# A decoder step's gate/up projection as seven block products instead of eight, and the down projection as a stage of its own

## The chip, the core and the metric

The program runs on one core of a Trainium2 chip. A core has TensorE (matrix products, PE in the profile), VectorE (DVE), ScalarE (ACT) and GpSimd (POOL), which work beside each other on a memory of 128 partitions (SBUF), with eight banks of PSUM for TensorE's sums; SyncE (SP) issues DMAs here, as does ScalarE. The metric is the device time of one launch in microseconds; less is better. Three runs of the kernel before took 3131.83, 3137.9 and 3143.32 us, median 3137.9.

## The reference

One layer of a decoder for a prompt of 2048 tokens and for 8 x 4 decoded tokens, in float32: an input projection, three branches of windowed attention, a state-space mixer, an output projection, a gated feed-forward part, and norms. What matters here:

```python
h = x + mixed @ w_out
gu = rmsnorm(h, norm_ffn) @ w_gate_up            # [tokens, 1024] @ [1024, 2 * 2816]
y = h + (silu(gu[:, :2816]) * gu[:, 2816:]) @ w_down
y = rmsnorm(y, norm_final)
```

## The kernel before

The prompt goes through in two halves of 1024 tokens, each as two quarters of 512. `half_step` (from L1131) runs the mixers and the output projection of the first quarter (its rows go to hD in DRAM), then of the second, and then the feed-forward part for both. The 32 decoded tokens go with the second half.

TensorE computes in a shortened form of float32, so each operand is split into a high and a low part, and each product is three matmuls (`mm3`, L102 to L109): high x high, high x low, low x high. A strip of weights of 128 columns is split where it arrives (`wunit`, L82 to L97: the high part on ScalarE, the low one on VectorE), and so are the inputs: `norm_T` (L125) normalizes 128 rows, transposes them on TensorE (L141) and splits them (L143, L144) into the tiles xa, for the first quarter, and xb.

The feed-forward loop (from L1312) runs over 22 groups f of 128 of the 2816 columns. For each group, the gate strip and then the up strip are multiplied with all blocks of tokens, 8 x 3 matmuls a block: in the first half two blocks of 512, in the second two of 272 (512 prompt tokens and the decoded ones) and one of 512. ScalarE takes the gate's silu (L1325), VectorE multiplies by the up sums (L1348), and the product is split (L1349, L1350). `down` (L1283 to L1301) then multiplies it with 128 rows of w_down and adds the sums to the eight accumulator rows acc (L1299): for each f in the first half, for two at a time in the second. TensorE thus changes between gate/up and down all through the stage. The decoded tokens' mixers are cut into some 60 steps (`sample_steps`), and `beside` puts up to three of them beside each f of the first half. Copies of cache rows from DRAM to DRAM are issued one per f. The next quarter's input is made ahead of the last `down` of the first half, and the last `down` carries the final norm (`finals`).

The order on an engine follows from a scheduler that takes the instructions by their place in the program and by when their inputs are ready; PSUM banks are asked for by name ("mm", "s", "o", "t").

Of the kernel before, what the change touches and what calls it, by code (L numbers as in the profile page):

```python
# [33 lines left out]
def hybrid_step(ctx: ExitStack, tc: tile.TileContext, x_prompt, x_sample, cache_kv_d1, cache_kv_d4,  # L34
# [33 lines left out]
    qD = dram.tile([NS, 768], F, name="qD")  # L68

# [12 lines left out]
    def wunit(src, a, pool=None, more=None):  # L82
        """[128, a, 1024//a] of a weight, as an exact sum of two fp32r parts; more: the parts of further columns"""
# [5 lines left out]
        hi, lo = [pool.tile([128, 1072 if pool is wsp else 1024], R, name=s)[:, :w].rearrange("p (a c) -> p a c", a=a)  # L89
                  for s in ("hi", "lo")]  # L90
# [11 lines left out]
    def mm3(ps, pairs):  # L102
        """sum over the pairs ((sh, sl), (mh, ml)) of s.T @ m"""
# [77 lines left out]
    def sample_state(sp):  # L181
        """constants and intermediates of the decoded tokens"""
# [50 lines left out]
    def x_stage(qi, xnp, es, nb=2):  # L233
        """-> the tiles of a quarter's input, and what makes the i-th of its rows' tiles"""
# [48 lines left out]
    def mixers(qi, xh, xl, mix, rssd, cvp):  # L283
# [15 lines left out]
        def g1(hi, lo, raw, M=128):  # L299
            """the strip's columns of the projection, by blocks of tokens: (psum, first, number)"""  # L300
# [6 lines left out]
        # weights, in the order they are used; each is asked for ahead of its use  # L307
# [25 lines left out]
        # ---- attention  # L333
# [4 lines left out]
        def softmax(mask, nk, hd_of, stt):  # L338
            """rows of scores -> unnormalized weights, negated maxima and sums in stt"""
# [63 lines left out]
        def kout(src_of, dst):  # L403
            """128 columns of a branch's two key strips as rows of the output"""
# [57 lines left out]
            # values, tokens on partitions  # L462
# [24 lines left out]
            # units  # L487
# [46 lines left out]
            # rows of the output  # L534
# [21 lines left out]
        # ---- state-space part  # L556
# [128 lines left out]
        # ---- gate of the state-space part, and its norm  # L685
# [445 lines left out]
    def half_step(half, X, right):  # L1131
# [51 lines left out]
        if not smp:  # L1183
            junk = g2.tile([128, D], F, name="j3")
# [313 lines left out]
```

## Time and profile before

| | |
|---|---|
| median of three runs | 3137.9 us |
| span of the profiled execution | 3141.2 us |
| TensorE busy | 3083.8 us (98%) |
| VectorE, ScalarE, GpSimd busy | 1649.3, 1075.0, 74.9 us |
| feed-forward, first half (775 to 1608) | 833.0 us |
| feed-forward, second half (2361 to 3134) | 773.0 us |
| mean DMA rate | 104 GB/s |

Instructions on TensorE are pipelined: the length shown for one is more than the distance to the next start, and the distance is what it costs. The profiled execution's own time is its span of 3141.2 us, 3.3 us above the median of the runs. The mean granted clock of TensorE is 0.986 of full speed.

### The profile page before, as it was taken

What the parts mean: (1) busy time and instruction counts of PE and PEld (TensorE: products, weight loads), DVE (VectorE), ACT (ScalarE), POOL (GpSimd) and SP (SyncE); (2) the same over time, 40 slices, a digit from 0 to 9 for tenths busy, and PEclk for the clock granted to TensorE, in tenths of its full rate; (3) what the DMA queues carried; (4) which work ended last, traced back from release to release, by engine and by line L of the source; (5) the groups of instructions that cost most, each with busy time, mean ns of one, the idle gap of its engine ahead of it and who ended that gap; (6) DMA issues with size and microseconds to landing.
All of it is one profiled execution on the core that took longest, in us unless ns stands there. A gap on an engine that the chain in (4) does not pass through costs nothing.

```text
span 3141.2 us, 44468 instructions
## 1 busy us (share of the span) xinstructions
PE 3083.8 (98%) x18203; PEld 2538.0 (81%) x18203; DVE 1649.3 (53%) x3186; ACT 1075.0 (34%) x2139; POOL 74.9 (2%) x106
## 2 busy tenths in 40 slices
PE   8999999999999999999999999999999999999999
PEld 7989877787768787787876787777878888888887
DVE  3359623796357466564553597237954333333334
ACT  3466424664221212121134564246633111111112
POOL 1000100000000000000000001000000000000000
PEclk9999999999989999999999999999999999999999
DMA  4323444343335344342244244443432111111111
GB/s 129 97 82 109 159 128 121 92 160 117 103 120 182 111 154 141 117 122 65 79 147 135 81 118 168 143 127 92 146 127 81 41 41 41 47 48 47 43 46 56
DMA packets 393391, 326.58 MB, mean 104 GB/s; under 512 B 51652, under 2 KB 357468, under 8 KB 392676
## 3 DMA queue, kind: packets, MB, share of 16 engines
q1 hardware_dynamic: 268688, 204.43, 21.4%
q10 hardware_dynamic: 124500, 119.31, 12.4%
q8 instruction: 143, 2.34, 0.3%
q14 instruction: 60, 0.49, 0.0%
HBM read 292.66 MB, written 58.16 MB: 112 GB/s over the span
## 4 chain that ended last, share of the span: by engine, by line
PE 90%; DMA 4%; DVE 3%; ACT 2%; issue 1%; ACTq 0%; POOL 0%; SPq 0%; POOLq 0%; DVEq 0%
PE mm L106 18%; PE mm L108 18%; PE mm L107 17%; PE s L106 4%; PE s L108 4%; PE s L107 4%; PE t L106 3%; PE t L107 3%; PE t L108 3%; PE o L106 3%; PE o L108 3%; PE o L107 3%; PE s L357 1%; DMA out<-ko 1%; PE t L364 1%; PE o L371 1%
## 5 line engine op out<-in xcount | busy, mean ns | idle before, releaser
L93 DVE TENSOR_TENSOR lo<-raw,hi 128x1024 fp32r<-128x1024 f32 x288 | 355.2, 1234 | 432.3 <-ACT hi L92 427.2
L92 ACT ACTIVATE hi<-raw 128x1024 fp32r<-128x1024 f32 x288 | 304.1, 1057 | 574.8 <-PE mm L107 260.3
L106 PE MATMUL mm<-xh,hi 128*128 128x512 f32 (+1 forms) x1280 | 469.2, 367 | 1.2 <-ACT xh L143 0.6
L108 PE MATMUL mm<-xh,lo 128*128 128x512 f32 (+1 forms) x1280 | 463.4, 362 | 1.1 <-DVE lo L93 1.1
L107 PE MATMUL mm<-xl,hi 128*128 128x512 f32 (+1 forms) x1280 | 460.6, 360 | 0.8 <-DVE xl L144 0.8
L1299 DVE TENSOR_TENSOR acc<-acc,t 128x512 f32<-128x512 f32 x264 | 180.7, 685 | 187.0 <-PE t L108 186.8
L108 PEld LDWEIGHTS mm<-xh,lo 128*128 128x128 f32 x1280 | 245.9, 192 | 40.6 <-issue 5.2
L106 PEld LDWEIGHTS mm<-xh,hi 128*128 128x128 f32 x1280 | 246.0, 192 | 38.8 <-issue 7.5
L107 PEld LDWEIGHTS mm<-xl,hi 128*128 128x128 f32 x1280 | 246.2, 192 | 34.2 <-issue 3.6
L106 PE MATMUL mm<-ha,hi 128*128 128x512 f32 (+1 forms) x704 | 243.5, 346 | 1.1 <-ACT ha L143 0.8
L108 PE MATMUL mm<-ha,lo 128*128 128x512 f32 (+1 forms) x704 | 241.6, 343 | 0.0
L107 PE MATMUL mm<-ha,hi 128*128 128x512 f32 (+1 forms) x704 | 240.7, 342 | 0.0
L1299 DVE TENSOR_TENSOR acc<-acc,o 128x512 f32<-128x512 f32 x264 | 180.3, 684 | 76.7 <-PE o L108 76.7
L106 PE MATMUL mm<-hb,hi 128*128 128x512 f32 x528 | 211.0, 400 | 0.0
L108 PE MATMUL mm<-hb,lo 128*128 128x512 f32 x528 | 207.6, 393 | 0.0
L107 PE MATMUL mm<-hb,hi 128*128 128x512 f32 x528 | 207.3, 393 | 0.0
L1335 ACT ACTIVATE m0h<-m0h 128x1024 fp32r<-128x1024 f32 x33 | 35.0, 1061 | 392.4 <-PE o L108 378.1
L106 PEld LDWEIGHTS mm<-ha,hi 128*128 128x128 f32 x704 | 133.0, 189 | 18.8 <-issue 2.2
L108 PEld LDWEIGHTS mm<-ha,lo 128*128 128x128 f32 x704 | 133.0, 189 | 16.3 <-DVE lo L93 0.4
L107 PEld LDWEIGHTS mm<-ha,hi 128*128 128x128 f32 x704 | 133.3, 189 | 15.3
L582 DVE SCALAR_TENSOR_TENSOR acc<-u,cw,acc 128x512 f32<-128x512 f32 x168 | 125.7, 748 | 3.5 <-ACT acc L580 1.8
L108 PEld LDWEIGHTS mm<-hb,lo 128*128 128x128 f32 x528 | 99.2, 188 | 24.0
(448 smaller groups left out, 6181.4 us busy)
## 6 DMA issues: line engine op xcount, KB each, us to landing
raw<-in_w_in SPq DMA_DIRECT2D x152, 512.0 KB
raw<-in_w_gate_up SPq DMA_DIRECT2D x88, 512.0 KB
raw<-in_w_out SPq DMA_DIRECT2D x48, 512.0 KB
m0h<-in_w_down SPq DMA_DIRECT2D x33, 512.0 KB
bc<-acD ACTq DMA_DIRECT2D x32, 384.0 KB
xt<-in_x_prompt SPq DMA_DIRECT2D x16, 512.0 KB
sk<-qD ACTq DMA_DIRECT2D x16, 512.0 KB
sk<-in_cache_kv_d ACTq DMA_DIRECT2D x16, 512.0 KB
```

Source lines behind the costliest of these rows:

```text
L92: nc.scalar.activation(h, raw, AF.Copy)
L93: nc.vector.tensor_tensor(l, raw, h.bitcast(F), op=OP.subtract)
L106: nc.tensor.matmul(ps, sh, mh, start=i == 0, stop=False)
L107: nc.tensor.matmul(ps, sh, ml, start=False, stop=False)
L108: last = nc.tensor.matmul(ps, sl, mh, start=False, stop=i == n - 1)
L357: nc.tensor.matmul(sb[a][:, 256 * i:256 * i + nk], q_of(i)[r], k_of(i)[r], start=True, stop=True)
L364: nc.tensor.transpose(tp[:, 128 * h:128 * h + 128], p[:, h, 128 * kb:128 * kb + 128], ident)
L371: nc.tensor.matmul(ops[64 * a:64 * a + 64, 128 * i:128 * i + 128], v_of(kb)[:, 64 * h:64 * h + 64], pT[:, kb, h, :], start=kb == 0, stop=k ...
L582: nc.vector.scalar_tensor_tensor(acc, u(j), w(j), acc, op0=OP.mult, op1=OP.add)
L1299: add = nc.vector.tensor_add(acc[i][:, ns], acc[i][:, ns], ps)
L1335: nc.scalar.activation(wd[0], wd[2], AF.Copy)
```

## The change

For 1024 tokens in a half, the normalized input is cut into four blocks, by quarter (1, 2) and by half of the 1024 inputs, and the gate and up strips likewise into halves of the inputs. The 2x2 block product of [first quarter; second quarter] with [gate, up] then takes seven products with sums of blocks in place of eight. The sums of the inputs (t1 to t4) are made on rows, before the transposition, on VectorE and GpSimd (`pair`), and each is transposed and split like a block (`put`, `part`). The sums of the weights (s1 to s4) are made per f on GpSimd (`prep_rest`, four operations) and split on ScalarE and VectorE (`split_unit`). `lead` runs two of the products of a round, `rest` the other five. A round has 512 tokens of each quarter in the first half; in the second, 528 (the decoded tokens are shared out by 16) go as two rounds of 264. The gated product is split and written to hiD and loD in DRAM.

A second stage then runs all of the down projection: eight groups of 2, 3, 3, 3, 3, 3, 3 and 2 f, whose activations are read back and whose products are summed in PSUM over the group. The accumulator rows are read from hD, where the second quarter's rows are now written as well; the decoded tokens' steps lie beside this stage alone, eight per group. The output projection runs its passes by halves of the inputs first. The diff also takes out comments and sets one build option (a smaller scratch for DMA descriptors).

```diff
-        s, half, u = i // 6, i // 3 % 2, i % 3
+        half, s, u = i // 6, i // 3 % 2, i % 3
...
         def after(ph):
-            norm_T(acc[ph], 128, gb, junk if ph % 2 else j2, xa[0], xa[1], 128 * ph)
+            normalize(ra[ph])
+            for h, k in enumerate(("11", "21")):
+                put(k, ra[ph][:, 512 * h:512 * h + 512], ph)
...
+            nc.vector.tensor_tensor(a[:, L], b[:, L], a[:, L], op=OP.subtract)
+            nc.gpsimd.tensor_tensor(b[:, L], b[:, H], b[:, L], op=OP.subtract)
+            nc.vector.tensor_tensor(b[:, H], b[:, H], a[:, L], op=OP.subtract)
+            nc.gpsimd.tensor_tensor(a[:, H], b[:, H], a[:, H], op=OP.subtract)
...
+            nc.gpsimd.tensor_tensor(s1, r2[:, L], r2[:, H], op=OP.add)
+            nc.gpsimd.tensor_tensor(r2[:, L], r1[:, L], r2[:, L], op=OP.subtract)
+            nc.gpsimd.tensor_tensor(r1[:, L], s1, r1[:, L], op=OP.subtract)
+            nc.gpsimd.tensor_tensor(r1[:, H], r1[:, H], r1[:, L], op=OP.subtract)
+            s2, s4 = split_unit(r1, 1024)
+            s3, a22 = split_unit(r2, 1024)
+            U["b", f] = s2, split_unit(s1, 512)[0], s3, s4, a22
...
+            for k in range(4):
+                for s, m in ((w[0], x[0]), (w[0], x[1]), (w[1], x[0])):
+                    last = nc.tensor.matmul(ps[:, :n], s[:, k], m[:, k, cs], start=start and k == 0 and s is w[0]
+                                            and m is x[0], stop=k == 3 and s is w[1], skip_group_check=True)
...
+            product(b1, a11, "11", c0, n, True)
+            nc.scalar.copy(ev[:, 0, :n], b1[:, :n])
+            b2 = bank("s")
+            product(b2, a12, "21", c0, n, True)
+            nc.vector.tensor_add(ev[:, 0, :n], ev[:, 0, :n], b2[:, :n])
+            nc.scalar.activation(ev[:, 0, :n], ev[:, 0, :n], AF.Silu)
...
+            product(b1, s2, "t2", c0, n, False)
+            nc.scalar.copy(e[1], b1[:, :n])
+            b3 = bank("o")
+            product(b3, s1, "t1", c0, n, True)
+            nc.scalar.copy(e[3], b3[:, :n])
+            product(b1, s3, "t3", c0, n, False)
+            nc.vector.tensor_add(e[3], e[3], b1[:, :n])
+            nc.scalar.copy(e[2], b1[:, :n])
+            product(b3, s4, "22", c0, n, False)
+            nc.vector.tensor_add(e[1], e[1], b3[:, :n])
+            act = nc.scalar.activation(e[1], e[1], AF.Silu)
+            nc.vector.tensor_mul(e[3], e[3], e[1])
+            b4 = bank("t")
+            product(b4, a22, "t4", c0, n, True)
+            nc.vector.tensor_tensor(e[2], e[2], b4[:, :n], op=OP.subtract)
+            nc.vector.tensor_mul(e[2], e[2], e[0])
...
+            nc.scalar.activation(hi.bitcast(R), lo, AF.Copy)
+            nc.vector.tensor_tensor(lo.bitcast(R), lo, hi, op=OP.subtract)
+            for t, p in ((hiD, hi), (loD, lo)):
+                dma2.dma_start(t[128 * f:128 * f + 128, :, c0:c0 + n], p)
...
+        for j, r in enumerate(rounds):
+            prep_rest(r[0])
+            if j + 1 < len(rounds):
+                lead(rounds[j + 1])
+            if j + 2 < len(rounds):
+                prep_lead(rounds[j + 2][0])
+            copy_rows(rest(r))
...
+        sizes = [2, 3, 3, 3, 3, 3, 3, 2]
...
+                for t, d in zip(A[j], (hiD, loD)):
+                    dma.dma_start(t.bitcast(F), d[128 * f:128 * f + 128, :, :TQ])
...
+                    if not after and nh:
+                        beside(sdk if not smp else None)
...
-        down(prev, finals)
+        ws = down_load(0)
+        for i in range(8):
+            dma2.dma_start(acc[i], hD[row(i):row(i) + 128])
+        dma2.dma_start(gf, bcast_rows(norm_final, D))
+        for g in range(len(sizes)):
+            last = g == len(sizes) - 1
+            if not last:
+                nw = down_load(g + 1)
...
+            down(ws, finals if last else None)
+            ws = nw
```

The order of instructions changes at these places. First TensorE at the head of the first half's feed-forward part: before, the second token block's transpositions (L141; m0l are its normalized rows here) and those of a first step of the decoded tokens (L843) stand between the gate matmuls of the first block, ha, and those of the second, hb.

```order
L106 MATMUL mm<-ha_7491,hi 128x512
L107 MATMUL mm<-ha_7492,hi 128x512
L108 MATMUL mm<-ha_7491,lo 128x512
L843 MATMUL s<-ident,sk 24x128 x3
L141 MATMUL t<-ident,m0l_7977 128x128 x4
L843 MATMUL s<-ident,sk 24x128
L141 MATMUL t<-ident,m0l_7977 128x128 x4
L843 MATMUL s<-ident,sk 24x128 x4
L106 MATMUL mm<-hb_7973,hi 128x512
L843 MATMUL s<-ident,sk 24x128 x4
L107 MATMUL mm<-hb_7974,hi 128x512
L108 MATMUL mm<-hb_7973,lo 128x512
```

After, the last matmuls of the two leads (x21) are followed by transposed pieces of t1, t3 and t4 (rb and ra are rows), and then the products with t2 begin.

```order
L1379 MATMUL s<-x21l,hi 128x512
L1280 MATMUL t<-ident,rb_7440 128x128 x4
L1379 MATMUL s<-x21h,lo 128x512
L1280 MATMUL t<-ident,rb_7441 128x128 x4
L1280 MATMUL t<-ident,rb_7442 128x128 x4
L1280 MATMUL t<-ident,ra_7435 128x128 x4
L1280 MATMUL t<-ident,ra_7436 128x128 x4
L1280 MATMUL t<-ident,ra_7437 128x128 x4
L1280 MATMUL t<-ident,ra_7438 128x128 x4
L1379 MATMUL mm<-xt2h,hi 128x512
L1379 MATMUL mm<-xt2l,hi 128x512
L1379 MATMUL mm<-xt2h,lo 128x512
```

Where one matmul or two stood between transpositions, there are now 24 transpositions in a row ahead of the first product with t2.

Next, ScalarE in the second half's feed-forward part, before: splits of activations (L1349) and weights (L92), and the gate's silu (L1325).

```order
L1349 ACTIVATE ah<-sg 128x272 x2
L1354 COPY sa<-sg 128x32
L92 ACTIVATE hi<-raw 128x1024
L1349 ACTIVATE ah<-sg 128x512
L1325 ACTIVATE sg<-s 128x272
L1325 ACTIVATE sg<-mm 128x272
L92 ACTIVATE hi<-raw 128x1024
L1325 ACTIVATE sg<-s 128x512
```

After, a round's stretch there: splits of weights (L1344), silu (L1413), the split of the gated product (L1422), the two writes to DRAM (L1425) and the copies of PSUM banks (L1404, L1407, L1391, L1410; ev is the round's tile).

```order
L1413 ACTIVATE ev<-ev 128x264
L1344 ACTIVATE hi<-s_23469 128x512
L1422 ACTIVATE ev<-ev 128x2x264
L1344 ACTIVATE hi<-raw 128x1024
L1425 DMA hiD<-ev 256x1x264
L1425 DMA loD<-ev 256x1x264
L1404 COPY ev<-mm 128x264
L1407 COPY ev<-o 128x264
L1391 COPY ev<-mm 128x264
L1410 COPY ev<-mm 128x264
```

The copies that free the banks for the next products now stand behind two DMAs that wait for VectorE's and ScalarE's parts of the round before.

Last, the loads of the accumulator rows. Before, SyncE asks for them at the start of the second quarter's output projection (L1190, L1192; here in the second half).

```order
L85 DMA raw<-in_w_out 128x2x512
L1190 DMA acc_19957<-in_x_prompt 128x1024
L1190 DMA acc_19958<-in_x_prompt 128x1024
L1190 DMA acc_19959<-in_x_prompt 128x1024
L1190 DMA acc_19960<-in_x_prompt 128x1024
L1192 DMA acc_19953<-hD 128x1024
L1192 DMA acc_19954<-hD 128x1024
L1192 DMA acc_19955<-hD 128x1024
L85 DMA raw<-in_w_out 128x2x512
L1192 DMA acc_19956<-hD 128x1024
L85 DMA raw<-in_w_out 128x2x512 x9
```

After, ScalarE asks for them behind the last round's gating (L1422) and its two writes (L1425), at the start of the down stage.

```order
L1422 ACTIVATE ev<-ev 128x2x264
L1425 DMA hiD<-ev 256x1x264
L1425 DMA loD<-ev 256x1x264
L1533 DMA acc_26037<-hD 128x1024
L1533 DMA acc_26038<-hD 128x1024
L1533 DMA acc_26039<-hD 128x1024
L1533 DMA acc_26040<-hD 128x1024
L1533 DMA acc_26041<-hD 128x1024
L1533 DMA acc_26042<-hD 128x1024
L1533 DMA acc_26043<-hD 128x1024
L1533 DMA acc_26044<-hD 128x1024
L1534 DMA gf<-in_norm_final 128x1024
```

They moved from SyncE's queue, one output projection and one gate/up stage ahead of their first use, to ScalarE's queue, right ahead of it.

## Rows read from the trace of the kernel before

**Rows 1.** The page: span; busy us by engine (share) xinstructions; chain by engine

```profile
span 3141.2 us, 44468 instructions
PE 3083.8 (98%) x18203; PEld 2538.0 (81%) x18203; DVE 1649.3 (53%) x3186; ACT 1075.0 (34%) x2139; POOL 74.9 (2%) x106
...
PE 90%; DMA 4%; DVE 3%; ACT 2%; issue 1%; ACTq 0%; POOL 0%; SPq 0%; POOLq 0%; DVEq 0%
```

**Rows 2.** Stretches: us, busy us by engine (instructions), clock, DMA share, GB/s

```profile
775.00:1608.00 833.00, 824.49 (x3896) 639.85 (x3897) 477.62 (x776) 183.36 (x281) 6.88 (x12) 0.98 0.37 118
830.00:902.00 72.00, 68.98 (x316) 44.99 (x315) 35.56 (x97) 14.55 (x28) 0.00 (x0) 0.79 0.42 136
2361.00:3134.00 773.00, 772.31 (x4438) 669.09 (x4435) 285.56 (x416) 145.53 (x252) 6.38 (x12) 1.00 0.15 48
...
1910.00:1920.00 10.00, 10.00 (x49) 8.29 (x48) 4.56 (x7) 2.12 (x2) 2.08 (x2) 1.00 1.01 374
2019.00:2024.00 5.00, 1.58 (x22) 0.82 (x20) 0.00 (x0) 1.91 (x3) 0.00 (x0) 1.00 0.75 256
2024.00:2031.00 7.00, 6.33 (x32) 3.56 (x30) 2.15 (x10) 2.12 (x9) 0.00 (x0) 0.53 0.59 189
```

**Rows 3.** Timelines of TensorE: start us, length us, engine, line, operation

```profile
755.56 1.03 PE L141 MATMUL t<-ident,j 128*128 128x128 f32 x8
756.35 0.47 PE L106 MATMUL mm<-hi,m1h 128*128 128x512 f32 x1
...
2449.81 0.29 PE L106 MATMUL mm<-ha,hi 128*128 128x272 f32 x1
...
2453.09 0.29 PE L108 MATMUL s<-ha,lo 128*128 128x272 f32 x1
...
2559.61 0.40 PE L108 MATMUL s<-hb,lo 128*128 128x512 f32 x1
...
2561.90 0.39 PE L106 MATMUL s<-hb,hi 128*128 128x512 f32 x1
```

**Rows 4.** Groups by line and shape, 775 to 1608: busy us, mean ns, idle

```profile
L1299 DVE TENSOR_TENSOR acc<-acc,o 128x512 f32<-128x512 f32 x176 | 119.7, 682 | 18.0 <-PE o L108 18.0
L1299 DVE TENSOR_TENSOR acc<-acc,t 128x512 f32<-128x512 f32 x174 | 118.8, 683 | 135.4 <-PE t L108 135.2
...
L93 DVE TENSOR_TENSOR lo<-raw,hi 128x1024 fp32r<-128x1024 f32 x45 | 54.8, 1217 | 1.0 <-ACT hi L92 0.9
...
L1348 DVE TENSOR_TENSOR m0l<-m0l,mm 128x512 f32<-128x512 f32 x44 | 30.2, 687 | 107.1 <-PE mm L108 106.9
L1350 DVE TENSOR_TENSOR m0l<-m0l,m0l 128x512 fp32r<-128x512 f32 x44 | 29.2, 685 | 4.1 <-ACT m0l L1349 3.9
...
L1336 DVE TENSOR_TENSOR m0h<-m0h,m0h 128x1024 fp32r<-128x1024 f32 x21 | 25.6, 1220 | 2.0 <-ACT m0h L1335 2.0
...
L144 DVE TENSOR_TENSOR hb<-t,hb 128x512 fp32r<-128x512 f32 x8 | 5.2, 685 | 1.0 <-ACT hb L143 1.0
...
L143 ACT ACTIVATE hb<-t 128x512 fp32r<-128x512 f32 x8 | 4.8, 594 | 3.9 <-PE t L141 3.9
...
L135 DVE SCALAR_TENSOR_TENSOR m0l<-acc,rstd,m0l 128x1024 f32<-128x1024 f32 x2 | 2.6, 1285 | 0.3 <-POOL rstd L114 0.2
```

**Rows 5.** The same view, 2361 to 3134

```profile
L1350 DVE TENSOR_TENSOR al<-sg,ah 128x272 fp32r<-128x272 f32 x44 | 19.5, 442 | 20.5 <-ACT ah L1349 20.4
```

**Rows 6.** Instructions of line 702: xcount, ns shortest/median/longest

```profile
L702 POOL TENSOR_TENSOR sq<-sq,acc x25: 706/1298/2239, 301.2 to 2281.8; 128x512 f32<-128x512 f32 x15, 128x272 f32<-128x272 f32 x5, 128x240 f32<-128x240 f32 x5
```

**Rows 7.** Timeline of GpSimd and VectorE, 670.5 to 674

```profile
671.05 1.30 POOL L702 TENSOR_TENSOR sq<-sq,acc 128x512 f32<-128x512 f32 x1 [286.90 <-issue]
...
671.18 2.25 DVE L93 TENSOR_TENSOR lo<-raw,hi 128x1024 fp32r<-128x1024 f32 x1
```

**Rows 8.** The chain that ended last: start us, us, what

```profile
1586.40 4.02 DMA xt<-in_x_prompt
...
1912.89 8.40 DMA xt<-in_x_prompt
```

More of the change, by code (lines that the diff above doesn't have):

```diff
@@ L795, in out_proj @@
         for ph in range(4):
-            s, half = ph // 2, ph % 2
+            half, s = ph // 2, ph % 2
             cs = slice(512 * s, 512 * s + 512)
@@ L1246, in after, with put @@
+        def put(k, src, i):
+            ps = bank("t")
+            p3 = ps.rearrange("p (k t) -> p k t", k=4)
+            for kk in range(4):
+                nc.tensor.transpose(p3[:, kk], src[:, 128 * kk:128 * kk + 128], ident)
+            part(k, p3, 128 * i, 128)
         def after(ph):
-            norm_T(acc[ph], 128, gb, junk if ph % 2 else j2, xa[0], xa[1], 128 * ph)
+            normalize(ra[ph])
+            for h, k in enumerate(("11", "21")):
+                put(k, ra[ph][:, 512 * h:512 * h + 512], ph)
@@ L1252, in half_step, with done2, f @@
+        def done2(i):
+            def f(cs):
+                dma2.dma_start(hD[row(4 + i):row(4 + i) + 128, cs], rb[i][:, cs])
+                if i and cs.stop == D:
+                    pair(i - 1)
+            return f
+        ol = [(128 * i, rssd[:, i:i + 1], rb[i], done2(i)) for i in range(4)]
         out_proj(ol, m2, rms, pre, wop, after, sample, residuals)
         es.close()
-        hB = open_pool(hnx, "hB", 1, side="right")
-        xb = [hB.tile([128, 8, TQ], R, name=f"hb{i}") for i in range(2)]
@@ L1268, in half_step, with beside, copy_rows @@
-        if smp:
-            nes.close()
-        grp = 2 if smp else 1
-        side = ExitStack()
+        steps = None if smp else sample_steps()
+        aes = ExitStack()
+        def beside(pool):
+            step = next(steps, None) if steps else None
+            if step:
+                step(pool, pool)
+        def copy_rows(ins):
+            if cps:
+                o, i = cps.pop()
+                with tc.issue_after(ins):
+                    dma2.dma_start(o, i)
+        ring = [0, None]
@@ new lines, in half_step @@
+        cuts = [(0, NB // 2), (NB // 2, NB // 2)] if smp else [(0, NB)]
+        rounds = [(f, c0, n) for f in range(NF) for c0, n in cuts]
+        blocks_of(open_pool(hx, "hC", 1, side="right"), ("t2", "t1", "t3", "t4"))
+        for k in ("22", "t1", "t2", "t3", "t4") if smp else ():
+            part(k, sample_b[k], TQ, NS // 2)
+        prep_lead(0)
+        pair(3)
+        for k, (t, c) in (("t2", (rb, H)), ("t1", (ra, L)), ("t3", (rb, L)), ("t4", (ra, H))):
+            for i in range(4):
+                put(k, t[i][:, c], i)
@@ L1274, in half_step @@
+        fes.close()
+        accp = open_pool(main, "accp", 1)
+        acc = [accp.tile([128, D], F, name=f"acc{i}") for i in range(8)]
+        fin = open_pool(main, "fin")
+        gf = fin.tile([128, D], F, name="gf")
+        sq_ = fin.tile([128, D], F, name="fsq")
+        ringA = open_pool(main, "dA", 1)
+        bes, side = ExitStack(), ExitStack()
+        ringB = open_pool(bes, "dB", 1, side="right")
         if not smp:
             sdk = open_pool(side, "sdk", 1)
-        steps = None if smp else sample_steps()
@@ L1301, in down @@
                     after(i, add.ins)
-        def proj(w, x, c0, n):
-            c0 = c0 if x is xa else c0 - TA
-            cnt[0] += 1
-            ps = bank("s" if smp and cnt[0] % 2 else "mm")
-            mm3(ps[:, :n], [((w[0][:, k], w[1][:, k]), (x[0][:, k, c0:c0 + n], x[1][:, k, c0:c0 + n]))
-                            for k in range(8)])
-            return ps
-        def beside():
-            step = next(steps, None) if steps else None
-            if step:
-                step(sdk, sdk)
@@ L1399, in finals @@
                     dma.dma_start(groups(y_sample.rearrange("b s d -> (b s) d"), a), q3(oS)[:, a])
-        down(prev, finals)
+        nxt = None
+        ws = down_load(0)
[6 more added lines that the diff above has]
+                nw = down_load(g + 1)
+            else:
+                for step in steps or ():
+                    step(sdk, sdk)
+                side.close()
+                bes.close()
+                if half == 0:
+                    nr = first_pools()
+                    with ExitStack() as xes:
+                        X2, stage = x_stage(2, nr[2], xes)
+                        for i in range(4):
+                            stage(i)
+                    nxt = X2, nr
+                if smp:
+                    for a in range(2):
+                        dma2.dma_start(q3(gq)[:, a], dap(norm_final, 512 * a, [[128, 4], [0, NS], [1, 128]]))
+            down(ws, finals if last else None)
+            ws = nw
         main.close()
```

259 lines of the change are left out of this document (140 added, 119 removed).

## The prediction

> **What bounds the kernel now.** I read the page's shares first: TensorE is busy for 3083.8 of 3141.2 us, and the chain that ended last runs over it for 90%; VectorE stands at 53%, ScalarE at 34%, GpSimd at 2% [rows 1]. So time goes only where TensorE gets less work, or stands still more. Next, busy time by stretch [rows 2]: the gate/up and down projections take 775 to 1608 in the first half (833.0 us, TensorE busy 824.5) and 2361 to 3134 in the second (773.0, busy 772.3). The clock is granted in full there (1.00), and at 0.98 in the first half, with a dip to 0.79 in 830 to 902. Then the pitch, from start to start, in a timeline of TensorE alone [rows 3]: ten steps of 512 columns from 2559.61 to 2561.90 give 0.229 us, 26 steps of 272 columns from 2449.81 to 2453.09 give 0.126. (The 0.39 and 0.29 shown for one are its length in a pipeline, not what it costs.) The second half's 1056 gate/up and 1056 down instructions of 512 and 2112 of 272 come to 484 + 266 = 750 of its 773 us: no idle time is to be won, only instructions.
>
> **Matmuls.** A block of 512 tokens takes 22 groups x 2 strips x 8 x 3 = 1056 instructions before. In the first half 2 x 1056 become 22 x 7 x 12 = 1848, still of 512 columns: -264 x 0.229 = -60.5 us. In the second, 1056 of 512 (-241.8) and 2112 of 272 (-266.1) become 22 x 2 x 7 x 12 = 3696 of 264, whose pitch the trace doesn't have: in proportion to 272 it is 0.1223, on a line through 272 and 512 it is 0.1226. I take 0.1225, +452.8, so -55.1. Together **-116**. The down projection keeps 1056 in each half.
>
> **Transposes.** The differences t1 to t4 need 96 more of 128x128. Eight stand in 755.56 to 756.35 [rows 3], 0.099 each: **+9.5**.
>
> **The head of each feed-forward stage.** Before, the gate matmuls start on the first token block while the second is still normalized and transposed. Now the row of TensorE has two leads (48 instructions, 11.0 us in the first half) and then most of the 16 transposed pieces of t2, t1, t3, t4 in a bunch, before the first product with t2. A piece costs VectorE 0.685 and ScalarE 0.594 [rows 4]. Behind the last sum of the output projection come a normalization (1.285), a piece of "22", two subtractions (0.685 each) and 16 x 0.685: 14.3 us of VectorE. The leads cover 11.0 of it, in the second half (264 columns) 5.9. That leaves 3.3 + 8.4, with a little for the GpSimd operation in the chain: **+14** (ends 0, with VectorE started early, and 45, both chains bare with the weights' splits of 1.217 ahead).
>
> **From gate/up to down.** The eight accumulator rows are asked for on ScalarE's queue behind the last round's writes to hiD and loD, so none leaves before the last gating, and ScalarE's copies for the last round stand ahead of them too. They are 4.2 MB, the norm row 0.5, the next group of three 4.7: some 9.4 MB, 25 us at 374 GB/s, the best stretch [rows 2]. Pieces of 512 KB took 4.0 and 8.4 us to land [rows 8]. The first down sums have the PSUM banks as their only cover. After a stop of TensorE, busy 1.58 of 5 us from 2019, the granted clock was 0.53 over the next 7 us [rows 2], near the lower of its two levels (1.2 of 2.4 GHz). I take 8 for each half, **+16** (ends 4, one landing hidden in part, and 45, the whole 25 us bare less the banks' cover).
>
> **Decoded tokens' steps.** In the first half they lie beside both stages before: TensorE's busy 824.5 less 3168 x 0.229 = 725.5 leaves 99 us for them, the next quarter's transposes and the dip of the clock; VectorE's 477.6 less 238.5 for the sums, 54.8, 30.2, 29.2 and 25.6 for splits and gating [rows 2, 4] leaves 99. All of it now lies beside the down stage, 1056 x 0.229 = 242 us and with its own matmuls some 310. VectorE there has 128 sums in place of 352, since a group of two or three column groups is summed in PSUM first: 87, plus 27 for splits, plus 99: 213 of 310. That fits on average, but steps that wait for cache rows now come twice as thick. 72 us at a clock of 0.79 cost 15 us; I take one more such loss: **+15** (ends 0 and 80; the rival below has the reason for the upper).
>
> **Rounds.** A round's products run through few banks: the third (s3 x t3) goes on in the bank that ScalarE must first copy, and one product lies between, 12 x 0.229 = 2.7 us in the first half, 1.5 in the second. ScalarE's row in the second half shows what can stand ahead of that copy: a split's high part of 128x1024, and the issue of loD, which waits for VectorE's low part (1.22). VectorE itself has per column group 3.5 splits (4.3 us) and 5.3 of gating of a round's 19.3 us in the first half; with 264 columns (0.442 for 272 [rows 5]) 2 x 3.4 + 4.3 of 20.6. It isn't the bound, but late by chance. I take 0.25 us in each of 22 + 44 rounds: **+16** (ends 0 and 86).
>
> Other edits count as nothing: the second quarter's rows written to hD and read again (2 MB each way per half beside matmuls), hiD and loD themselves (46 MB in 880 us of gate/up, where the window now moves 48 to 118 GB/s of 374), the order of the output projection's passes (same instructions), the smaller DMA scratch. The tail's covers grow from one column group's down to two.
>
> **Sum.** -116 + 9.5 + 14 + 16 + 15 + 16 = -45.5. The profiled execution's span is 3141.2, 3.3 above the median 3137.9 of the runs; the difference carries over: **3092 us** for a run.
>
> **Rivals.**
> *A, nearly all of it arrives.* VectorE and ScalarE are half idle, and the second half's stretch keeps the DMA engines at a share of 0.15 [rows 2], so loads can run ahead. With heads, transitions, steps and rounds at 4, 6, 0 and 4: 3137.9 - 116 + 9.5 + 14 = 3045. Against it: two new hand-overs where one engine waits for a chain.
> *B, the first half's down stage is bound by loads.* hiD, loD and w_down are 1.5 MB per column group, 34.6 MB with their twins in all, the accumulators 4.7, and the steps' caches and states, in and out, some 31 (98 MB of the window [rows 2], less 66 strips of 0.52 and 6 for rows in and out, less some 25 of cache rows copied through): 70 MB. At 374 GB/s that is 188 us and hidden; at 189, as in 2024 to 2031 [rows 2], 370, 60 above the stage's 310. The upper end less the 15 taken: 3137, no change. For it: reads of keys and values come in a bunch there.
> *C, GpSimd holds VectorE.* Each column group's four sums run on GpSimd, 1.298 us each, from SBUF (the median of such operations [rows 6]). In the trace one at 671.05 to 672.35 stands beside a split of VectorE that began at 671.18 and took 2.25 us instead of the usual 1.22 [rows 4, 7]: it lost 1.03, as if it had begun when the other ended. With 88 of them in each half, VectorE's low parts come late, loD's issue holds ScalarE, and the PSUM copies are late by one whole operation in each round: 66 x 1.3 = 86, in place of 16: 3137.9 + 24.5 = 3162, **slower**. It decides from (45.5 + 16) / 66 = 0.93 us per round. Against it: VectorE is only half used, and of a round's sums at most two fall on a split that is due at once.
> The Trainium skill, "SBUF — State Buffer", section "SBUF: two separate sides", calls the pair of ports that VectorE and GpSimd share an exclusive lock: of a VectorE operation with two SBUF inputs and a GpSimd one, whoever starts first has it for the whole instruction. By that rule the trace's 2.25 is the general case.
> *D, the change doesn't do what it says:* matmuls of 264 columns keep the pitch of 272 or worse, and at 0.126 the second half saves 42, not 55: 3106 and up.
>
> **Chances.** Forecast 0.50 (its own range 3062 to 3122), A 0.20, B 0.13, C 0.13, D 0.04. Below 3128.5 or above 3147.3, 0.3% of the median, counts as a difference, about what a measurement can tell. The forecast, A and D are faster, with a small part of B: 0.78; most of B and a little of C is the same: 0.09; C and the worst of B slower: 0.13. Range 3035 to 3152.
>
> **What would show it.** Windows of the gate/up stages: TensorE busy near 423 and 453 us, with idle time of 0.25 us per round put down to ScalarE's copies or VectorE's sums. A gap of 3 to 9 us ahead of the first product with t2, and of some 8 ahead of the first down sum, released by a DMA into acc. The first half's down stage at 300 to 325 us. Wrong would be: splits of VectorE at 2.2 us beside GpSimd throughout with TensorE's idle time behind them (C), a stage above 350 us that waits for cache rows (B), or stages without such gaps (A).

## The result: slower

The changed kernel takes 3191.2 us (median of four runs, 3185.6 to 3195.9), the kernel before 3138.6 on the same chip: a ratio of 1.016, interval 1.0144 to 1.0182: a loss of 1.6%, clear of the noise. The forecast was 3092 with a range up to 3152, so it missed the time and the sign. The profiled execution has a span of 3183.7 us, 42.5 above the 3141.2 of [rows 1]; it is the fastest of its four runs, so some 10 of the 52.6 us between the medians aren't in what follows.

The page of the changed kernel, engines and then the chain that ended last:

```profile
PE 3021.9 (95%) x18563; PEld 2513.0 (79%) x18563; DVE 1762.6 (55%) x3314; ACT 1244.5 (39%) x2463; POOL 364.0 (11%) x298
...
PE 77%; DMA 9%; DVE 7%; ACT 3%; issue 2%; POOL 1%; ACTq 1%; SPq 0%; POOLq 0%; DVEq 0%
```

TensorE's busy time fell by 62 us against [rows 1], but its share of the chain fell from 90% to 77%: DMA, VectorE and ScalarE took 19% in place of 9%. Its mean granted clock fell too, from 0.986 to 0.969. By stretch (us, busy us of TensorE, its weight loads, VectorE, ScalarE and GpSimd, then clock, DMA share, GB/s), the gate/up and down stages of the first half, the second half's gate/up, and the start of that:

```profile
783.00:1230.00 447.00, 441.32 (x1915) 356.26 (x1916) 231.04 (x259) 185.22 (x259) 135.53 (x88) 0.99 0.49 162
1230.00:1621.00 391.00, 346.95 (x1744) 251.13 (x1743) 229.35 (x419) 66.19 (x129) 6.49 (x12) 0.90 0.60 198
2384.00:2906.00 522.00, 483.71 (x3783) 473.98 (x3785) 284.15 (x449) 217.29 (x425) 130.16 (x92) 0.96 0.29 93
...
2384.00:2410.00 26.00, 18.43 (x103) 15.18 (x101) 18.55 (x30) 11.02 (x23) 13.10 (x10) 0.78 0.31 91
```

The second half's down stage is what is left, 2906 to 3183.7. With the matmuls at the forecast's pitches (423 and 453 us for gate/up, 242 for each down stage), what each stage takes beyond them is this; the stretches of before are those of [rows 2], the second one taken to the end of the span.

| beyond the matmuls, us | before | after | more | forecast |
|---|---|---|---|---|
| gate/up, first half: 447 - 423 | | 24 | | |
| gate/up, second half: 522 - 453 | | 69 | | |
| down, first half: 391 - 242 | | 149 | | |
| down, second half: 277.7 - 242 | | 36 | | |
| both halves: 833 - 725.5, 780 - 750 | 137.5 | 278 | 140.5 | 70.5 |
| up to the first gate matmul of each half | 1528 | 1546 | 18 | 0 |

140.5 + 18 - 116 = 42.5. So if the 116 us came in, 158 us of new waiting, work and low clock stand against them, where the forecast had 70.5. That they came in rests on the program's counts and on the pitch of 264 columns, which is in the trace now, 27 steps:

```profile
2734.80 0.28 PE L1379 MATMUL mm<-x11l,hi 128*128 128x264 f32 x1
...
2738.09 0.28 PE L1379 MATMUL mm<-xt2l,hi 128*128 128x264 f32 x1
```

0.1219, against 0.1225 in the sum.

### The profile page after: what moved, and what is told of

Same layout as the page of the kernel before. It is cut to its first block, busy times and chain, and to the rows that moved or that the text cites. A ratio compares the mean times of both kernels' runs of the same rounds, so it can differ in the third digit from the quotient of the medians.

```text
span 3183.7 us, 46691 instructions
## 1 busy us (share of the span) xinstructions
PE 3021.9 (95%) x18563; PEld 2513.0 (79%) x18563; DVE 1762.6 (55%) x3314; ACT 1244.5 (39%) x2463; POOL 364.0 (11%) x298
## 4 chain that ended last, share of the span: by engine, by line
PE 77%; DMA 9%; DVE 7%; ACT 3%; issue 2%; POOL 1%; ACTq 1%; SPq 0%; POOLq 0%; DVEq 0%
PE mm L1379 10%; PE mm L108 9%; PE mm L110 9%; PE mm L109 9%; PE o L1379 7%; PE t L1379 3%; PE s L1379 3%; PE t L108 2%; PE o L109 2%; PE o L110 2%; PE t L109 2%; PE o L108 2%; PE t L110 2%; DMA raw<-in_w_down 2%; DMA sk<-qD 1%
## 5 line engine op out<-in xcount | busy, mean ns | idle before, releaser
L94 ACT ACTIVATE hi<-raw 128x1024 fp32r<-128x1024 f32 x222 | 233.7, 1057 | 531.8 <-DVE acc L1501 126.3
L1501 DVE TENSOR_TENSOR acc<-acc,t 128x512 f32<-128x512 f32 x128 | 87.6, 685 | 126.3 <-PE t L110 110.1
L1501 DVE TENSOR_TENSOR acc<-acc,o 128x512 f32<-128x512 f32 x128 | 87.6, 684 | 85.0 <-PE o L110 84.8
L1345 DVE TENSOR_TENSOR lo<-sum,hi 128x1024 fp32r<-128x1024 f32 x66 | 92.0, 1394 | 66.1 <-ACT hi L1344 66.0
L108 PE MATMUL mm<-hi,xh 128*128 128x256 f32 (+3 forms) x408 | 115.6, 284 | 0.5 <-ACT vt L474 0.5
L109 PE MATMUL mm<-lo,xh 128*128 128x256 f32 (+3 forms) x408 | 116.0, 284 | 0.0
L110 PE MATMUL mm<-hi,xl 128*128 128x256 f32 (+3 forms) x408 | 115.9, 284 | 0.0
L1379 PE MATMUL mm<-xt3h,hi 128*128 128x264 f32 (+1 forms) x264 | 88.1, 334 | 23.9 <-ACT ev L1404 23.9
L349 ACT ACTIVATE p<-p,st 128x256 f32<-128x256 f32 (+4 forms) x192 | 83.8, 440 | 63.2 <-DVE st L347 56.7
L1423 DVE TENSOR_TENSOR ev<-ev 128x528 fp32r<-128x528 f32 (+1 forms) x66 | 75.3, 1142 | 46.6 <-ACT ev L1422 45.4
L1422 ACT ACTIVATE ev<-ev 128x528 fp32r<-128x528 f32 (+1 forms) x66 | 51.8, 785 | 115.7 <-DVE ev L1418 98.0
```

Of the source, the lines that this page charges most:

```text
L94: nc.scalar.activation(h, raw, AF.Copy)
L108: nc.tensor.matmul(ps, sh, mh, start=i == 0, stop=False)
L109: nc.tensor.matmul(ps, sh, ml, start=False, stop=False)
L110: last = nc.tensor.matmul(ps, sl, mh, start=False, stop=i == n - 1)
L349: nc.scalar.activation(p[:, h, :nk], p[:, h, :nk], AF.Exp, bias=stt[:, h:h + 1], accum_out=stt[:, 4 + h:5 + h])
L1345: nc.vector.tensor_tensor(lo[:, :n], src, hi[:, :n].bitcast(F), op=OP.subtract)
```

## Experiments

Each ratio below is to the kernel before on the same chip, since its median moved from 3138.6 to 3143.2 between chips; 0.01 is 31 us. A stage's length is read from one profiled execution of each kernel.

**The steps left out, of both kernels.** In each, the steps' generator is not made, and the mixed values they would give are set to a constant.

```diff
+        nc.vector.memset(mS, 0.5)
...
+        nc.vector.memset(rS, 0.5)
...
-        steps = None if smp else sample_steps()
+        steps = None
```

> The kernel before without the decoded tokens' steps (their mixers are left out, their mixed values are set to a constant). Base for the next run. Both theories: the 99 us that TensorE has beside its projections in the first half's feed-forward part go, less the next quarter's transposes: 3045 to 3060 us.

> The changed kernel without the decoded tokens' steps (left out in the same way). Theory S (the steps, crowded into the first half's down stage, are the main loss): that stage falls from 391 us to 255 to 275 with its hand-over, the whole to 3055 to 3075, and against the kernel before without steps it is no more than 20 us slower instead of 53. Rival R (the loss is in the rounds and hand-overs of both halves): the steps take as much time from both kernels, so it stays 45 to 60 us slower than the kernel before without steps, some 3100.

Before without steps: 3059.7 us, 0.974 (0.9719 to 0.9754). After without steps: 3066.4, 0.976 (0.9739 to 0.978). The steps cost the kernel before 80 us and the changed one 125, and without them the two kernels are nearly level, 7 us apart. So some 45 of the 52 us go with the steps (theory S). But S isn't all: of the 116 us of saved matmuls nothing is left even without steps, so some 120 us go elsewhere (the 116 and the 7, the transposes' 9.5 among them). The first half's down stage of the changed kernel without steps, and behind the "..." a stretch of that stage with them:

```profile
1235.00:1506.00 271.00, 253.48 (x1102) 205.43 (x1103) 132.94 (x185) 43.49 (x58) 5.49 (x10) 0.97 0.48 169
...
1290.00:1330.00 40.00, 40.00 (x214) 23.59 (x212) 22.92 (x70) 6.12 (x18) 0.00 (x0) 0.79 0.35 103
```

271 against 391, and the clock at 0.97 against 0.90. A loss of clock of 0.07 over 391 us is 27 us. From 1290 to 1330 TensorE never stopped, with the state steps' small matmuls among its own, and had 0.79; in each 40 us from 1250 to 1410 it had 0.79 to 0.85, for longer than the dip of [rows 2] (72 us at 0.79). The other part of the loss is waiting. What TensorE and VectorE waited for in this stage with the steps (us, times, longest):

```profile
PE o L108 <- DVE acc L1501: 17.6, 5, 6.6
PE t L108 <- DVE acc L1501: 13.7, 2, 10.7
...
DVE sk L992 <- DMA sk<-qD: 25.7, 10, 4.7
```

TensorE is idle for 44 of the 391 us. For 31 of them, 10.7 at the hand-over, it waits for a bank that VectorE has still to add to the accumulator rows (L1501). The longest of the others, 6.6 us, on VectorE and then on TensorE:

```profile
1367.97 1.23 DVE L992 TENSOR_TENSOR sk<-sk 128x1024 f32<-128x1024 f32 x1 [3.96 <-DMA sk<-qD]
1369.12 0.68 DVE L1501 TENSOR_TENSOR acc<-acc,o 128x512 f32<-128x512 f32 x1
...
1369.85 0.80 PE L108 MATMUL o<-wh,ah 128*128 128x512 f32 x1 [6.60 <-DVE acc L1501]
```

VectorE stands for a load of the steps, and the accumulator sum that frees the bank comes behind. Without the steps TensorE is idle for 17.5 us, 13.4 of them such a wait.

**The sums of weights on VectorE.** `nc.gpsimd` becomes `nc.vector` in the four lines of `prep_rest`.

```diff
-            nc.gpsimd.tensor_tensor(s1, r2[:, L], r2[:, H], op=OP.add)
+            nc.vector.tensor_tensor(s1, r2[:, L], r2[:, H], op=OP.add)
...
```

> The changed kernel with the four sums of each column group's weights on VectorE instead of GpSimd. Theory G (GpSimd's sums, 1.3 to 2.0 us each in a chain of four, and the port they hold, make VectorE's and ScalarE's parts of a round late): the second half's gate/up stage falls from 521 us to 485 to 500, its stalls ahead of the third product from 24 us to under 8, the first half's from 448 to about 442; the whole 25 to 40 us faster than the changed kernel (3150 to 3165). Rival (VectorE, with 4 x 0.69 more for each column group, is late by itself): within 10 us of the changed kernel or slower.

3152.8 us, 1.0034 (1.0019 to 1.0049): 40 us faster than the changed kernel, 34 of it in the second half's gate/up stage (522 to 488):

```profile
2382.00:2870.00 488.00, 469.63 (x3776) 462.41 (x3775) 302.74 (x533) 218.98 (x423) 9.50 (x8) 0.99 0.31 100
```

Theory G holds at the upper end of its range for the time. The first half's stage, expected at 442, went from 447 to 451: with rounds of 512 columns the sums on GpSimd cost nothing that this run gives back. The trace of the changed kernel shows how the sums held TensorE up. What TensorE waited for in the second half's stage (us, times, longest):

```profile
PE mm L1379 <- ACT ev L1404: 23.9, 13, 3.5
```

And one of these waits, a timeline of GpSimd, VectorE and ScalarE in the changed kernel (start us, length us, engine):

```profile
2575.99 1.97 POOL L1366 TENSOR_TENSOR s<-sum 128x512 f32<-128x512 f32 x1 [13.49 <-DMA sum<-in_w_gate_up]
...
2576.74 1.27 DVE L1420 COPY sa<-ev 128x32 f32<-128x32 f32 x1
...
2578.11 1.79 DVE L1423 TENSOR_TENSOR ev<-ev 128x528 fp32r<-128x528 f32 x1
...
2579.29 1.73 POOL L1368 TENSOR_TENSOR raw<-s,raw 128x512 f32<-128x512 f32 x1
...
2579.93 0.52 ACTq L1425 DMA_DIRECT2D loD<-ev  x1
...
2581.10 1.26 POOL L1369 TENSOR_TENSOR raw<-raw 128x512 f32<-128x512 f32 x1
...
2582.40 1.06 ACT L1344 ACTIVATE hi<-raw 128x1024 fp32r<-128x1024 f32 x1 [5.97 <-DMA loD<-ev]
...
2583.36 0.36 ACT L1404 COPY ev<-mm 128x264 f32<-128x264 f32 x1
```

A copy of 32 columns took 1.27 us beside a GpSimd sum, and the split of the gated product 1.79. ScalarE's split of the sums comes ahead of the copy that frees TensorE's bank (L1404), and it starts only when the fourth sum has ended, at 2582.36. (The view puts ScalarE's 5.97 us down to loD's issue, but that left at 2579.93; the next run but one settles it.) From 2420 to 2850, groups of the changed kernel and then of the one with the sums on VectorE (busy us, mean ns behind the comma):

```profile
L1423 DVE TENSOR_TENSOR ev<-ev 128x528 fp32r<-128x528 f32 x38 | 38.6, 1017 | 18.9 <-ACT ev L1422 17.7
...
L1420 DVE COPY sa<-ev 128x32 f32<-128x32 f32 x19 | 14.5, 763 | 0.5
```

```profile
L1423 DVE TENSOR_TENSOR ev<-ev 128x528 fp32r<-128x528 f32 x41 | 28.9, 706 | 19.3 <-ACT ev L1422 19.3
...
L1420 DVE COPY sa<-ev 128x32 f32<-128x32 f32 x20 | 3.5, 177 | 0.2
```

1017 against 706 ns, 763 against 177: VectorE's operations take longer beside GpSimd's sums. By the exclusive lock on a shared port pair that the Trainium skill describes ("SBUF — State Buffer", section "SBUF: two separate sides") this is to be expected of operations with two SBUF inputs, such as L1423, and of those in a 2-port mode, which the same section says a copy can enter. The trace agrees for L1423, and for the copy L1420 if it runs in that mode, which no trace shows. The run takes away two things at once, this hold and GpSimd's slower chain of four sums (6.4 us here; on VectorE a sum takes 0.69 us); how the 40 us divide between them isn't shown. A stop can also cost what comes behind it. The stop at 2580 and the 5 us after it in the changed kernel, and then a shorter one with what followed:

```profile
2580.00:2584.00 4.00, 0.52 (x4) 0.31 (x3) 0.51 (x1) 1.60 (x4) 2.29 (x2) 0.86 0.19 68
2584.00:2589.00 5.00, 5.00 (x24) 5.00 (x24) 1.48 (x3) 1.08 (x4) 0.00 (x0) 0.50 0.36 105
...
2606.80:2609.00 2.20, 0.98 (x8) 0.77 (x7) 0.53 (x1) 1.08 (x2) 2.12 (x2) 1.00 0.28 98
2609.00:2615.00 6.00, 6.00 (x52) 6.00 (x52) 4.32 (x8) 2.70 (x7) 0.82 (x1) 1.00 0.36 110
```

24 matmuls in 5 us at a clock of 0.50, the lower level; at 0.122 it would have been 41. A stop of 3.8 us cost some 6. Behind the shorter one the clock stayed at 1.00.

**The sums left out.** The strips are split in their place.

```diff
-            s2, s4 = split_unit(r1, 1024)
...
-            U["b", f] = s2, split_unit(s1, 512)[0], s3, s4, a22
+            U["b", f] = s2, split_unit(r2[:, L], 512)[0], s3, s4, a22
```

(The first line stays; the four sums above it and s1 go.)

> The changed kernel without the sums of weights: the strips themselves are split in their place, so the gate/up products leave the sums out. It shows the whole price of the sums. If VectorE carries them at little cost (theory G as it stands): the second half's gate/up stage at 480 to 488 us, as with the sums on VectorE (488), and the whole at 3143 to 3153. If the sums on VectorE cost much as well: 465 to 478 and 3115 to 3140.

3163.2 us, 1.0064 (1.0047 to 1.0081): with less work it is slower than with the sums on VectorE, the second half's gate/up stage 502 against 488. Neither expectation holds. TensorE waits there at another place, 12.5 us in eight times for ScalarE's copy of the other bank (L1407 in the changed kernel). In some rounds ScalarE's row stands in another order than with the sums on VectorE. That the scheduler's order is the whole reason for the 10 us is likely but not shown, and what the sums themselves cost can't be read from this run.

**The writes to hiD and loD by SyncE.**

```diff
-                dma2.dma_start(t[128 * f:128 * f + 128, :, c0:c0 + n], p)
+                dma.dma_start(t[128 * f:128 * f + 128, :, c0:c0 + n], p)
```

> The changed kernel with the writes to hiD and loD issued by SyncE instead of ScalarE. Theory Q (ScalarE stands at loD's issue until VectorE has the low part, and the copies that free the banks are behind it): the second half's gate/up stage falls from 521 us to 495 to 505, the whole to 3165 to 3176. Rival G (ScalarE waits in any case, for the sums of GpSimd that it has to split, and VectorE's low part is late for the port): 512 to 521, within 9 us of the changed kernel.

3194.3 us, 1.017 (1.0146 to 1.0195), the stage at 520: no change. The issue of loD, which the prediction named as what holds ScalarE, isn't the cause of the stage's loss. ScalarE's waits in this run (from 2420 to 2850):

```profile
ACT hi L1344 <- POOL raw L1369: 19.2, 6, 6.0
ACT hi L1344 <- POOL sum L1369: 18.1, 6, 6.0
```

With the DMAs gone from its queue, ScalarE stands for 37 us on GpSimd's last sum; in the changed kernel it was 10 us on that sum and 18 put down to loD's issue, the longest 6.0 us as here. That is rival G.

**The rows of the accumulators by SyncE.**

```diff
-            dma2.dma_start(acc[i], hD[row(i):row(i) + 128])
+            dma.dma_start(acc[i], hD[row(i):row(i) + 128])
```

> The changed kernel with the accumulator rows asked for on SyncE's queue, behind the first group's loads of the down stage and ahead of the second's, instead of on ScalarE's. Theory H (the first sums wait because the rows share the DMA engines with the second group's loads): TensorE's stops of 11.0 and some 7 us at the two hand-overs fall to 2 to 5 us, with the low clock behind them 12 to 25 us less in all (3166 to 3179). Rival (the rows can't leave earlier, for their place in memory is the old tiles'): the stops stay and the time is within 6 us of the changed kernel.

3197.7 us, 1.0165 (1.0139 to 1.0192): no gain. In the second half TensorE's stop fell from 8.1 to 4.0 us, since the first accumulator sum began 9.9 us behind the last gate matmul instead of 14.0, and yet the stage took 277.7 us as before. In the first half the requests left 12 us behind the last gate matmul instead of 13, and the first sum began some 19 us behind it instead of 20. There, in the changed kernel, ScalarE's split (behind a load) stood ahead of the requests and TensorE stopped for 10.7 us; the last two lines are the stretches of its two hand-overs:

```profile
1242.99 1.06 ACT L94 ACTIVATE hi<-raw 128x1024 fp32r<-128x1024 f32 x1 [5.86 <-DMA raw<-in_w_down]
...
1243.46 13.93 ACTq L1533 DMA_DIRECT2D acc<-hD  x8
...
1250.61 0.80 PE L108 MATMUL t<-wh,ah 128*128 128x512 f32 x1 [10.72 <-DVE acc L1501]
...
1230.00:1250.00 20.00, 7.66 (x38) 5.31 (x36) 7.42 (x10) 4.27 (x5) 0.00 (x0) 0.87 0.96 350
2906.00:2920.00 14.00, 6.54 (x40) 4.69 (x32) 3.46 (x9) 0.90 (x2) 0.00 (x0) 0.91 1.02 360
```

The DMA engines are at a share of 0.96 and 1.02 through them. The stop isn't the steps' doing: in the changed kernel without steps the first half's is 11.9 us.

**Loads of the steps further ahead.** Three rows of keys or values, and two states, in nine buffers.

```diff
-SLOTS = 4
+SLOTS = 9
...
-            for b in range(7):
-                yield both(keys_load(br, b + 1), keys(br, b))
+            for b in range(8):
+                yield both(more(), keys(br, b))
```

(`more` gives the next load of all branches; three are issued ahead of the first keys.)

> The changed kernel with the decoded tokens' loads three rows of keys or values ahead of their use instead of one (two states instead of one; nine buffers instead of four). Theory L (a step now follows each 18 matmuls, about 4 us, and a load takes 5 to 10 us, so VectorE stands on loads with the accumulator sums queued behind): the first half's down stage falls from 391 us to 330 to 350, VectorE's waits for loads there from 26 us to under 8, the whole to 3135 to 3152. Rival B (the DMA engines are full in that stage): it stays above 378, and the time within 12 us of the changed kernel's 3191.

3189.5 us, 1.0148 (1.0132 to 1.0163), the stage at 388: theory L falls. Where stops of 6.6, 4.6 and 1.0 us had been, there is one of 19, and ScalarE, which issues these loads, stood 24.4 us. The DMA engines of this run from 1340 to 1382, in 40 slices, their busy share in tenths and then the rate:

```profile
DMA  0485001468989999999999999999999500266784
GB/s 0 162 290 141 0 31 57 124 239 260 325 294 359 375 374 378 377 375 369 357 355 373 386 387 376 361 352 347 349 349 337 173 20 0 16 218 265 113 324 147
```

```profile
ACT hi L94 <- DMA sk<-in_cache_kv_d: 24.4, 1, 24.4
```

For some 19 us they move 347 to 387 GB/s at nine tenths and more: they are full, and asking earlier gives no more of them. ScalarE's split of the next group's weights stands behind the loads that it is to issue.

**Fewer bytes, and the bytes spread.** One kernel leaves out the loads of the queries (the scores are then made from the keys alone); in the other, nothing is left out and a step is given 1 to 3 places, by its bytes, with twice as many places as before.

```diff
-                dmas.dma_start(qb[:nk], dap(qD, 4 * b * 768 + 256 * br, [[0, nk], [768, 4], [1, 256]]))
```

```diff
-                    if not after and nh:
+                    if not after:
                         beside(sdk if not smp else None)
...
+        w = [2] * 8
+        for br in range(3):
+            w += [(2, 3, 2)[br]] * 9 + [(1, 2, 1)[br]] * 8
```

> The changed kernel without the loads that spread the decoded tokens' queries over the partitions (10 MB of the steps' 31; the scores are computed from the keys alone). All else stays, the lead of the loads too. Theory B (in the stretches of the keys' steps, 1.05 MB per step of 4.1 us and 4.7 MB per group of 33 us ask for some 400 GB/s, and the DMA engines give 350 to 378): the first half's down stage falls from 391 us to 340 to 360, VectorE's waits for loads in it to under 8 us, the whole to 3145 to 3165. Rival C (the loss there is the low clock after the hand-over and beside the state steps, with VectorE's and TensorE's own work for the steps): 380 or more.

> The changed kernel with the steps spread by their bytes: 6 us instead of 4 for a step of the second branch's keys, half as much for the values of the first and third. Nothing is left out. Theory B: the most that is asked for falls from 400 to about 310 GB/s, and the stage from 391 to 355 to 375, the whole to 3160 to 3178. Rival C: 385 to 395, no change in the time.

Without the queries' loads: 3176.6 us, 1.0117 (1.0101 to 1.0133), 14 us less, and VectorE's waits for these loads, 25.7 us in the changed kernel, are gone. The stage takes 373 us instead of 391:

```profile
1235.00:1608.00 373.00, 340.03 (x1745) 246.02 (x1745) 228.92 (x419) 66.70 (x130) 6.98 (x12) 0.91 0.55 179
```

That is the direction of theory B and half its size. Spread: 3189.3, 1.0156 (1.0141 to 1.0171), the stage at 388: no gain by itself, as rival C had it. The queries' bytes are worth 14 to 18 of the 45 us. Of the rest, the clock is a part (0.91 still, without those loads); how much, and what the steps' own work costs with less beside it, isn't shown.

**Two names of banks for the transposed pieces.**

```diff
         def put(k, src, i):
-            ps = bank("t")
+            nput[0] += 1
+            ps = bank("to"[nput[0] % 2])
```

> The changed kernel with the transposed pieces of the inputs put into two names of PSUM banks in turn instead of one. Theory P (in the bunch of 16 a piece takes 1.29 us, not the 0.69 of VectorE, since it waits for a bank that ScalarE and VectorE must both have read): the bunch falls to 0.75 to 0.95 a piece, the two heads cost 8 to 16 us less in all, 3175 to 3184. Rival V (VectorE is late by GpSimd's port and the splits, whatever the banks): within 6 us of the changed kernel.

3171.9 us, 1.0099 (1.0079 to 1.0119): 20 us less, more than expected; the two gate/up stages fall by 8 and 12. VectorE in the bunch of the second half, the changed kernel, then this one, and then the one with the sums on VectorE, which has one name of banks:

```profile
2413.17 0.69 DVE L1245 TENSOR_TENSOR xt3l<-t,xt3h 128x512 fp32r<-128x512 f32 x1 [0.22 <-ACT xt3h L1244]
2414.85 0.69 DVE L1245 TENSOR_TENSOR xt3l<-t,xt3h 128x512 fp32r<-128x512 f32 x1 [0.99 <-ACT xt3h L1244]
2415.70 0.69 DVE L1245 TENSOR_TENSOR xt4l<-t,xt4h 128x512 fp32r<-128x512 f32 x1 [0.16 <-ACT xt4h L1244]
```

```profile
2403.30 0.68 DVE L1245 TENSOR_TENSOR xt3l<-o,xt3h 128x512 fp32r<-128x512 f32 x1
2403.89 0.68 DVE L1245 TENSOR_TENSOR xt3l<-t,xt3h 128x512 fp32r<-128x512 f32 x1
2404.49 0.68 DVE L1245 TENSOR_TENSOR xt3l<-o,xt3h 128x512 fp32r<-128x512 f32 x1
```

```profile
2404.71 0.69 DVE L1245 TENSOR_TENSOR xt1l<-t,xt1h 128x512 fp32r<-128x512 f32 x1 [0.21 <-ACT xt1h L1244]
...
2413.11 0.69 DVE L1245 TENSOR_TENSOR xt4l<-t,xt4h 128x512 fp32r<-128x512 f32 x1 [0.20 <-ACT xt4h L1244]
```

Two pieces in 2.53 us before, one each 0.6 now: the pieces were bound by the two banks of one name, which TensorE, ScalarE and VectorE had to go through one after the other, not by VectorE's 0.685. Theory P. A part of it is TensorE's clock: it was 0.50 in the changed kernel's bunch (2410 to 2416) and 1.00 in the other two, and at 1.00 with two banks eight pieces take 8.40 us, 1.05 each. So of the 1.27 us some 0.2 go with the low clock and some 0.45 with the banks.

**Combinations.**

> The changed kernel with four edits: sums of weights on VectorE, loads of the decoded tokens three ahead, writes to hiD and loD by SyncE, and the copy of the decoded tokens' activations on ScalarE. If the losses add up (38 measured for the sums, some 45 for the lead, 0 to 10 for the rest): 3095 to 3112, 0.9% to 1.4% faster than the kernel before. If the DMA engines bound the first half's down stage: 3140 to 3155.

Sums on VectorE, loads ahead, writes by SyncE, the copy (L1420) on ScalarE: 3156.5, 1.0032 (1.0015 to 1.0049), as the sums alone.

> That, with the sums of weights on VectorE and the copy of the decoded tokens' activations on ScalarE. If theories G and B hold and add up: 3120 to 3140, the same as the kernel before or a little faster. If the stage stays at 390: 3150 to 3156, as with the sums on VectorE alone.

Sums on VectorE, steps spread, the copy on ScalarE: 3145.4, 1.0012 (0.9998 to 1.0027). Level with the kernel before. Against the sums alone it is 7 us less, with intervals that overlap; the spread stage took 384 us here where it took 388 alone, and 391 without the spreading.

> The last combination (sums on VectorE, steps spread by bytes, the copy on ScalarE; 3145) with the two names of banks and with the splits of the second down group queued on ScalarE behind the requests for the accumulator rows. If the heads fall and the stops of 8 us at the hand-overs do by half: 3122 to 3135, faster than the kernel before by 0.1% to 0.5%. If the rows can't leave earlier and the heads are bound by VectorE: 3140 to 3148.

That, with the two names of banks, and with ScalarE's splits for the second group behind the requests for the rows (`behind([accd[3].ins] if g == 0 else [])` around `down_load`): **3130.6 us, 0.9966 (0.9955 to 0.9978)**, 0.34% faster than the kernel before and 62 us faster than the changed one. The stops at the hand-overs stayed at 9.7 and 8.6 us, though the requests now left at 1234.9, 5 us behind the write of loD. The page, and the second half's gate/up stage:

```profile
PE 2997.5 (96%) x18563; PEld 2498.6 (80%) x18563; DVE 1817.5 (58%) x3468; ACT 1246.7 (40%) x2485; POOL 101.9 (3%) x122
...
2370.00:2850.00 480.00, 466.18 (x3777) 460.76 (x3775) 299.61 (x512) 219.15 (x444) 9.51 (x8) 1.00 0.32 102
```

480 of 522 us, at a full clock.

## Why the prediction was wrong, step by step

- **Matmuls and transposes** (-116, +9.5): right as far as measured. The pitch is 0.1219 where 0.1225 was taken, and TensorE is the engine that got less work. Its busy time fell by only 62 us, at the lower mean clock (0.969 for 0.986). What the 96 transposes cost by themselves no run shows.
- **The head** (+14): the mechanism was right, VectorE's and ScalarE's chain with TensorE bare, and the price too small. It counted 0.685 us for a piece; a piece took 1.27, for its banks and the low clock. It also looked only behind the first product: 18 us more lie ahead of it, put at nothing. In the first half TensorE's transpositions wait there for the normalized rows and their differences (7.8 us in four waits), in the second for those (1.2) and for the decoded tokens' rows (5.5). The two names of banks alone gave back 20.
- **From gate/up to down** (+16): the stops were 10.7 and 8.1 us, with the DMA engines at 350 to 360 GB/s, so the size was about right. The reason given, ScalarE's queue, is at best a part of it, and the fit is then partly luck: SyncE's requests halved the second half's stop without shortening its stage, and left the first half's; requests sent earlier on ScalarE left both. That the 9.4 MB take as long as the first group's 22 us of matmuls, and can't start before the old tiles' memory is free, fits these runs, but no run shows it by itself: open.
- **Decoded tokens' steps** (+15): failed; they cost 45. The prediction divided 70 MB by the whole stage and found it hidden. In the stretch of the keys' steps a step asks for 1.05 MB in 4.1 us and the group for 4.7 MB in 33: 400 GB/s by this estimate, more than the 347 to 387 that the engines gave when full. So VectorE stood for the steps' loads with the accumulator sums behind them, and TensorE was idle for 44 us of the stage. And the clock stood at 0.90 over the stage, at most 39 us, where the forecast had the dip of before, 15, and one more. Rival B came nearest on the stage, 370 for the 391 measured; its cause, the loads, is worth 14 to 18 us of that by the run without the queries. The upper end of 80 was left without a source, since rival B's working gives 60.
- **Rounds** (+16): failed; moving the sums off GpSimd alone gave back 40, and none of it in the first half's rounds. The copy that comes late and the bank behind it were named, and so was VectorE held by GpSimd (rival C). What was missed is the queue on ScalarE: its split stands on a chain of four GpSimd operations (6 us), ahead of the copies, and the clock fell to 0.50 behind a stop of 3.8 us. Rival C's 3162 had the right sign; it had a chance of 0.13. But its path, loD's issue holding ScalarE, isn't the cause: without that issue the stage stayed.
- **Chances**: of the four costs with a range, the forecast took 61 us; the middles of the ranges come to 130, the upper ends to 256. Measured were 149 (158.5 less the 9.5 for transposes). All four were taken near their low ends, and three came out high together. That they share one cause, the cover that TensorE lost when stages were taken apart, is a reading; no run tests it.

## What to carry to other kernels

Where one engine is busy for 98%, work taken off it comes back only if everything beside it still has cover: price a cut by the slack of the other engines and queues stage by stage, and by the shortest stretch, not by a stage's mean. Look at each in-order queue for what stands ahead of the instruction that frees the busy engine's bank, and follow that back over all engines. When several new waits may hang on one lost cover, don't take each near its low end: here the middles of their ranges would have come close.

## What was not expected of the hardware

- The prediction had priced VectorE's splits beside GpSimd; a copy of 128x32 on VectorE took 0.763 us on average beside GpSimd's sums and 0.177 without them.
- A stop of TensorE of 3.8 us was followed by 5 us at a clock of 0.50, and the clock was 0.79 over 40 us in which TensorE never stopped (1290 to 1330).
- The DMA engines gave 347 to 387 GB/s for some 19 us on end, with loads from two queues.
- A kernel with the sums left out was 10 us slower than one with them on VectorE. The scheduler's order of ScalarE's row is the likely reason, not a shown one.
